# The low part of the split weights of the last feed-forward: by an adding GpSimd transfer instead of a VectorE subtraction

## Chip, core and metric

The kernel runs on one core of a Trainium2 chip. The metric is the time of one execution on the device in microseconds (us); the time of a kernel is the median over its runs. Engines in the rows: PE is TensorE (PEld its weight loads), DVE is VectorE, ACT is ScalarE, POOL is GpSimd, SP is SyncE (SPq the queue that issues the loads).

## The reference, cut to what matters

One sequence of 512 tokens with 1024 features, in float32, goes through a first block (mixed attention and a feed-forward) and then a second block of two layers. Each layer of the second block ends in a feed-forward with 4096 hidden features; behind the last one stands a norm, which is the result:

```python
def sq_relu_mlp(h, w1, w2):
    return jnp.square(jax.nn.relu(h @ w1)) @ w2
...
        x = x + g2 * sq_relu_mlp(modulate(rms_norm(x, norm2_g[l]), sh2, sc2), w_mlp1[l], w_mlp2[l])
...
    return rms_norm(x, final_norm_g)
```

In the last layer (`l == 1`) the feed-forward has this one stream of 512 tokens.

## The kernel before

**Split products.** TensorE multiplies in `float32r`, which keeps fewer bits than float32. Each operand is therefore held as a high part, rounded to `float32r`, and a low part, the rest, and each product is made as three (`mm3`, lines 128 to 131): high weights with high tokens (L129), low weights with high tokens (L130), high weights with low tokens (L131).

**Weights.** `load_w` (lines 109 to 119) brings one weight tile of 128 x 1024 float32 (512 KB): SyncE loads it into `wstage` (L116), ScalarE copies it into `whi` (L117), and VectorE subtracts, `wlo = wstage - whi` (L118). On the lane "main" there are two buffers for `wstage` and three for `whi` and `wlo` each, handed out in the order of the program: a tile takes the buffers of the tile three before it, and waits until TensorE has read them for the last time.

**The last feed-forward** (`mlp`, from line 226). The 4096 hidden features are worked on in 8 groups of 512. A group has eight weight tiles, called A0 to A3 and B0 to B3 here. A0 to A3 are tiles of `w1`: 24 products of 512 columns each give 128 hidden features (`d`), which ScalarE takes through ReLU, square and the copy `uh` (L256, L260, L261) and VectorE into the low part `ul` (L262). B0 to B3 are tiles of `w2`: each gives two output tiles of 128 features, with the four hidden tiles of the group as inputs (`uh`, `ul`), 24 products again, and VectorE adds them to the residual stream (`area`, L287). 64 weight tiles in all. In the first group A0 to A2 go over the first 256 tokens and then the second 256, because the second half's norm comes later. In the last group B2 and B3 are done in halves of 256 tokens too, so that the final norm can start.

**What sets the order.** Nothing is ordered by hand here. A scheduler places all instructions on the engines' queues by priority and by a model of their times, and within an engine they run in that order; each waits for semaphores. `d` banks are seven in the last layer. GpSimd has the softmax's subtraction in the attention before (L744) and the final scaling (L1305), and issues no transfers.

Of the kernel before, what the change touches and what calls it, by code (L numbers as in the profile page):

```python
# [10 lines left out]
F32 = mybir.dt.float32  # L11
# [4 lines left out]
OP = mybir.AluOpType  # L16
# [12 lines left out]
# the parts that the tokens of a stream (0: x, 1: context) are worked on in where a norm would hold up the rest  # L29
# [17 lines left out]
def kernel(ctx: ExitStack, tc: tile.TileContext, A, out, dbg=None):  # L47
# [36 lines left out]
    # ---------------------------------------------------------------- helpers  # L84

    # Buffers of one name are handed out in program order. Work that shall overtake other work needs its own: a lane.
# [22 lines left out]
    def load_w(src, n, cuts=()):  # L109
        ln = lane[lane[""]]  # L110
        wst, width = ln["wst"], ln["width"]
        st = wst.tile([128, width], F32, name="wstage", bufs=ln.get("stage"))
        hi = wst.tile([128, width], F32R, name="whi", bufs=ln.get("split"))
        lo = wst.tile([128, width], F32R, name="wlo", bufs=ln.get("split"))
        for a, b in zip((0, *cuts), (*cuts, n)):
            nc.sync.dma_start(st[:, a:b], src[:, a:b])  # L116
            act.activation(hi[:, a:b], st[:, a:b], AF.Copy)  # L117
            dve.tensor_sub(lo[:, a:b], st[:, a:b], hi[:, a:b].bitcast(F32))  # L118
        return hi, lo

    def after(cur, prev):
        """cur is issued behind prev on the same engine."""
# [10 lines left out]
    def split(hi, lo, src, scale=None, shift=None):  # L133
        """hi + lo = src * scale + shift, each exact in float32r."""
# [16 lines left out]
    def rstd_steps(srcs, n, width, psum, name="n", parts=None, gains=None, ending=1):  # L151
        """In two pieces, the steps for the first sources and a call for the rest and the result:
        1 / sqrt(mean over features + eps), on every partition; srcs: [128, n] feature tiles. With parts: a list of
        calls, one per part of the tokens, that give it. With gains: of y = rms_norm(src) * gain, rms_norm(y) being
        src * gain times what the first such list gives, and y src * gain times what the second gives."""
# [18 lines left out]
        def rest():  # L174
            for sl in parts:
                for i in range(together, len(srcs)):
                    add(i, sl)
                if gains:
                    # 1 / (r1 r2)^2 = mean((x gain)^2) + eps / r1^2
# [26 lines left out]
    def normed(hT, srcs, rstd, scale, shift=None):  # L206
        """hT[k] (hi, lo) = srcs[k] * rstd * scale[k] (+ shift[k])"""
# [5 lines left out]
    def normed_stream(hT, v, psum, gain, shift, ending, rest=None):  # L213
        """normed for a whole stream, one part of its tokens after the other"""
# [5 lines left out]
    def by_parts(n_tiles, units, lead):  # L220
        """Order of work of weight tiles on units of tokens: the first tiles go through unit after unit, so that
        later units can still be on their way."""
# [3 lines left out]
    def mlp(streams, w1, w2, pool_u, psum, side=None, rstd=None, ending=1):  # L226
        """x[m] += gate(m) * (relu(h @ w1)^2 @ w2)[m] for each stream (x, hT, n, gate); h = hT (* rstd)"""
        parts = [PARTS[0 if st[2] == S else 1] for st in streams]
        for g in range(32 // GRP):
# [34 lines left out]
            # towards the end the tokens' parts come one after the other, for the norm behind  # L264
# [6 lines left out]
            for mb, mm, ci, sl in steps:  # L271
                if mb not in ws:
                    # the last weights have buffers of their own: the others are for what comes next
# [18 lines left out]
    # ---------------------------------------------------------------- residual streams  # L292
    # The first block needs its input for its first norm and again where it adds to it; in between, the memory
    # of the residual stream serves the modulations.
# [3 lines left out]
    # ---------------------------------------------------------------- work on the second block's weights alone  # L298
# [3 lines left out]
    def filling(behind=0):  # L302
        """Work for when nothing else is ready."""
# [5 lines left out]
    # shift1, norm1_g * (1 + scale1), gate1, shift2, norm2_g * (1 + scale2), gate2; one column per feature tile  # L309
# [5 lines left out]
    def modulations(held, passing, scratch, behind=None):  # L315
        """silu(c) @ w_mod + b_mod for both condition vectors, by products and sums along the free axis."""
# [42 lines left out]
    def filters(fp, psum, which):  # L359
        """Spectra of the long convolutions at the odd half frequencies, cosine and sine parts."""  # L360
# [78 lines left out]
    # ---------------------------------------------------------------- second block, one stream at a time  # L439
# [10 lines left out]
    def mixers(lq, n):  # L450
        """Fourier input, convolution gate, convolution input"""
        return [[lq.tile([128, n], F32, name=f"{nm}{i}") for i in range(2)] for nm in ("F", "x0_", "z")]

    def front_norm(pi, ps, l, v, rest=None):
        """Normed and modulated input."""
# [18 lines left out]
    def front(pi, ps, l, v, lat, mixin, hT):  # L474
        """The input's projections and their latents."""
# [13 lines left out]
        # the convolution's inputs come last: until then their tiles are free  # L489
# [35 lines left out]
        def conv(i, p, dst):  # L525
            """dst = short convolution of channel tile i along tokens"""
# [113 lines left out]
    def values(ap_, ps, l, key_lats):  # L640
        """Values of all heads, token-major."""
# [17 lines left out]
    def attention(ap_, sm, l, v, key_lats, lat, ps, es=None, lp=None, fill=()):  # L659
        """Latent attention of stream v over the keys of key_lats; its output, transposed, in four tiles, which may  # L660
        take the memory of the latents in lp. fill: pieces of other work on the tensor engine."""
# [5 lines left out]
        # the rotary rows of the keys are the same for every head  # L667
# [9 lines left out]
        def heads(j, ps):  # L677
            """queries and keys of a pair of heads"""
# [88 lines left out]
        # behind the rest of the attention in order: for when nothing of it is ready  # L767
# [6 lines left out]
    def out_half(l, half, src, v, ps):  # L774
        """x += gate * (four of the mix tiles) @ w_out"""
# [3 lines left out]
    def out_pieces(l, half, src, v, ending=4):  # L779
        """out_half in pieces, each with the pool of its sums' bank; those of the last weight tiles one part of the  # L780
        tokens after the other"""
# [26 lines left out]
    def side_lane(wrk, width=0, stage=0, split_=0, banks=3):  # L808
        """A lane of its own, with weight buffers where width is given."""
# [8 lines left out]
    def second_block_prologue(ph, ps):  # L818
        """Work that the first block's output has no part in: modulations, filters, the context's first layer
        up to its feed-forward. In pieces, for between the groups of the first block's feed-forward."""  # L820
# [5 lines left out]
        def side(g, j, load):  # L826
            at = 4 * g + j
            if at == BL:
                # the new schedule begins with weights at hand
# [64 lines left out]
    # ================================================================ block 1  # L894
    with ExitStack() as ph:
# [5 lines left out]
        # the norm's 1 / rms is applied to the projections  # L901
# [19 lines left out]
        # gated linear attention operands: bq, bk, br  # L921
# [32 lines left out]
        # relative position tables f_h(e - 127), kept in DRAM  # L954
# [13 lines left out]
        # values and gate inputs, token-major: av | cv | bv | ba  # L968
# [25 lines left out]
        # twelve causal heads; two per tile  # L994
        def head_pairs():
            for j in range(6):
# [6 lines left out]
                if j == 5:  # L1003
                    # all projections are made: the memory of their input is free
# [6 lines left out]
                for i in range(4):  # L1011
# [3 lines left out]
                    for h2 in range(2):  # L1015
                        h_ = 2 * j + h2
                        r = slice(64 * h2, 64 * h2 + 64)
                        # once the linear attention is through, its buffers serve every second head
                        other = gla_done and h2
                        p = ps1.tile([128, 512], F32, name="g" if other else "s")  # L1020
                        # float32r products of under 256 columns take longer than those of 256
# [31 lines left out]
        # log decay, cumulative within each 128-token tile, on [(head, key channel), token]  # L1053
# [34 lines left out]
        # Within a tile, a key meets a query at the level at which they part into the halves of one block: the decay  # L1088
        # between them is the product of the key's up to the middle and the query's from there. Level 0 is the diagonal.
# [7 lines left out]
        # the queries of a level, each head's in its own rows and columns: one product takes all heads  # L1097
# [49 lines left out]
        # states before tiles 1..3  # L1147
# [366 lines left out]
```

## Time and profile before

| | |
|---|---|
| runs | 2357.88 and 2352.8 us, median 2355.34 |
| profiled execution | span 2353.3 us (the page gives no other time of it) |
| busy in the span | TensorE 97%, VectorE 62%, ScalarE 42%, GpSimd 6% |
| share of the chain that ended last | TensorE 87%, VectorE 6%, DMA 3%, ScalarE 2% |
| transfers | 248.52 MB, all issued by SyncE but 0.4% of the engines' time |

The page sums up an execution; the share of an engine is an average over stages. The last feed-forward takes from about 1980 us to 2338 us of the span, the final norm the rest. What decides there is which wait ends last ahead of a product of TensorE, since TensorE has no gap between its products.

### The profile page before, as it was taken

What the parts mean: (1) busy time and instruction counts of PE and PEld (TensorE: products, weight loads), DVE (VectorE), ACT (ScalarE), POOL (GpSimd) and SP (SyncE); (2) the same over time, 40 slices, a digit from 0 to 9 for tenths busy, and PEclk for the clock granted to TensorE, in tenths of its full rate; (3) what the DMA queues carried; (4) which work ended last, traced back from release to release, by engine and by line L of the source; (5) the groups of instructions that cost most, each with busy time, mean ns of one, the idle gap of its engine ahead of it and who ended that gap; (6) DMA issues with size and microseconds to landing.
All of it is one profiled execution on the core that took longest, in us unless ns stands there. A gap on an engine that the chain in (4) does not pass through costs nothing.

```text
span 2353.3 us, 32927 instructions
## 1 busy us (share of the span) xinstructions
PE 2287.6 (97%) x12907; PEld 1898.1 (81%) x12907; DVE 1469.5 (62%) x2641; ACT 996.0 (42%) x1717; POOL 137.0 (6%) x173
## 2 busy tenths in 40 slices
PE   8999999999999999899999999999899999999997
PEld 7866677778877788788988888888878788888886
DVE  7888778576666684766785554533755666443345
ACT  5344553344344452654533322343443644333333
POOL 0022200000000000321000000000001220000000
PEclk9999999999999999999999999999999999999999
DMA  6523454434331422102354442321222101332232
GB/s 232 166 76 131 130 166 151 164 134 141 126 100 63 149 82 72 54 19 75 106 180 152 152 152 72 103 90 59 83 89 73 41 28 46 107 99 98 90 99 72
DMA packets 78853, 248.52 MB, mean 106 GB/s; under 512 B 9342, under 2 KB 13872, under 8 KB 77930
## 3 DMA queue, kind: packets, MB, share of 16 engines
q1 hardware_dynamic: 78698, 246.42, 31.9%
q8 instruction: 102, 1.67, 0.3%
q14 instruction: 53, 0.43, 0.1%
HBM read 241.63 MB, written 4.75 MB: 105 GB/s over the span
## 4 chain that ended last, share of the span: by engine, by line
PE 87%; DVE 6%; DMA 3%; ACT 2%; issue 1%; POOL 0%; SPq 0%; DVEq 0%; ACTq 0%; POOLq 0%
PE d L129 23%; PE d L130 22%; PE d L131 22%; PE o L760 3%; PE t L750 2%; DVE wlo L118 1%; PE s L129 1%; PE s L131 1%; DMA area<-in_wmod_dram 1%; PE e L129 1%; PE s L130 1%; PE e L429 1%; PE o L1042 1%; PE e L130 1%; PE e L131 1%
## 5 line engine op out<-in xcount | busy, mean ns | idle before, releaser
L117 ACT ACTIVATE whi<-wstage 128x1024 fp32r<-128x1024 f32 (+4 forms) x318 | 324.6, 1024 | 511.0 <-PE d L131 426.3
L118 DVE TENSOR_TENSOR wlo<-wstage,whi 128x1024 fp32r<-128x1024 f32 (+4 forms) x318 | 378.0, 1191 | 256.2 <-ACT whi L117 253.5
L129 PE MATMUL d<-uh,whi 128*128 128x512 f32 (+1 forms) x1056 | 380.4, 361 | 1.3 <-ACT uh L261 1.3
L130 PE MATMUL d<-uh,wlo 128*128 128x512 f32 (+1 forms) x1056 | 379.8, 360 | 0.0
L131 PE MATMUL d<-ul,whi 128*128 128x512 f32 (+1 forms) x1056 | 374.3, 359 | 0.0
L129 PEld LDWEIGHTS d<-uh,whi 128*128 128x128 f32 x1056 | 198.5, 188 | 33.8 <-ACT uh L261 2.2
L131 PEld LDWEIGHTS d<-ul,whi 128*128 128x128 f32 x1056 | 198.9, 188 | 32.4 <-issue 1.5
L130 PEld LDWEIGHTS d<-uh,wlo 128*128 128x128 f32 x1056 | 198.7, 188 | 30.9 <-issue 1.3
L287 DVE SCALAR_TENSOR_TENSOR area<-d,mod,area 128x512 f32<-128x512 f32 (+1 forms) x134 | 95.4, 725 | 145.2 <-PE d L131 145.1
L256 ACT ACTIVATE w<-d 128x256 f32<-128x256 f32 (+1 forms) x96 | 50.4, 525 | 215.9 <-PE d L131 209.2
L338 DVE SCALAR_TENSOR_TENSOR w<-wm,cb 128x1024 bf16<-128x1024 f32 x96 | 114.9, 1220 | 25.7 <-DMA wm<-in_wmod_dram 25.5
L262 DVE TENSOR_TENSOR ul<-w,uh 128x512 fp32r<-128x512 f32 (+1 forms) x128 | 79.3, 622 | 19.9 <-ACT uh L261 19.8
L338 DVE SCALAR_TENSOR_TENSOR mj<-area,area 128x1024 bf16<-128x1024 f32 x64 | 79.7, 1246 | 6.9 <-DMA area<-in_wmod_dram 6.1
L739 DVE TENSOR_REDUCE mx<-s 128x1 f32<-128x768 f32 x64 | 61.2, 956 | 33.6 <-PE s L131 32.8
L260 ACT ACTIVATE w<-w 128x512 f32<-128x512 f32 (+1 forms) x128 | 73.0, 570 | 6.5 <-DVE w L258 5.6
L261 ACT ACTIVATE uh<-w 128x512 fp32r<-128x512 f32 (+1 forms) x128 | 73.9, 577 | 3.5
L744 POOL TENSOR_SCALAR sb<-sb,mx 128x768 f32<-128x768 f32 x64 | 57.9, 906 | 207.7 <-DVE mx L740 80.4
L760 PE MATMUL o<-pt,V 128*64 128x128 f32 x768 | 64.9, 281 | 0.0
L285 DVE TENSOR_TENSOR area<-d,area 128x512 f32<-128x512 f32 (+1 forms) x66 | 44.2, 672 | 31.4 <-PE d L131 31.1
L750 PE MATMUL t<-c_ident,sb 128*128 128x128 f32 x384 | 60.7, 281 | 0.8 <-ACT pt L753 0.7
L674 POOL CAST k000h<-kr0h 32x512 fp32r<-32x512 f32 x2 | 1.7, 844 | 1017.9 <-PE d L625 1017.9
L287 DVE SCALAR_TENSOR_TENSOR ctx<-d,mod,ctx 128x256 f32<-128x256 f32 x64 | 30.8, 481 | 48.0 <-PE d L131 47.8
(1185 smaller groups left out, 5761.0 us busy)
## 6 DMA issues: line engine op xcount, KB each, us to landing
wstage<-in_w_m_dram SPq DMA_DIRECT2D x128, 512.0 KB, 3.5
wstage<-in_w_ff_dram SPq DMA_DIRECT2D x64, 512.0 KB, 4.2
wm<-in_wmod_dram SPq DMA_DIRECT2D x64, 512.0 KB, 4.2
wstage<-in_w_in_dram SPq DMA_DIRECT2D x56, 512.0 KB, 3.4
area<-in_wmod_dram SPq DMA_DIRECT2D x32, 512.0 KB, 4.2
wstage<-in_w_out_dram SPq DMA_DIRECT2D x32, 512.0 KB, 3.5
wstage<-in_w_v_dram SPq DMA_DIRECT2D x8, 520.0 KB, 4.2
ktab<-in_kt_dram SPq DMA_DIRECT2D x16, 256.0 KB, 2.7
```

Of the source, the lines that this page charges most:

```text
L117: act.activation(hi[:, a:b], st[:, a:b], AF.Copy)
L118: dve.tensor_sub(lo[:, a:b], st[:, a:b], hi[:, a:b].bitcast(F32))
L129: pe.matmul(ps, lhsT=whi, rhs=xhi, start=start, stop=False)
L130: pe.matmul(ps, lhsT=wlo, rhs=xhi, start=False, stop=False)
L131: pe.matmul(ps, lhsT=whi, rhs=xlo, start=False, stop=stop)
L260: act.activation(u, r, AF.Square)
L261: act.activation(uh, u, AF.Copy)
L262: mark[g, j] = dve.tensor_sub(ul, u, uh.bitcast(F32))
L287: dve.scalar_tensor_tensor(x[m][:, sl], ps, gate(m), x[m][:, sl], op0=OP.mult, op1=OP.add)
L338: after(dve.scalar_tensor_tensor(t, w, 1.0, sv[v], op0=OP.mult, op1=OP.mult, accum_out=mraw[l][v][j // 8][:, j % 8:j % 8 + 1]), behind)
L750: pe.transpose(pt[:, (kk - a) * 128:(kk - a + 1) * 128], sb[:, kk * 128:(kk + 1) * 128], ident)
L760: last_[h2] = after(pe.matmul(po[64 * h2:64 * h2 + 64, q], lhsT=V[kk][:, 64 * h_:64 * h_ + 64], rhs=PT[h2][:, kk * 128:(kk + 1) * 128], st ...
```

## The change

In the last layer's feed-forward, from its first weight tile on, the low part is made in two steps. ScalarE writes minus the high part into `wlo`: a copy of `wstage` with scale -1, rounded to `float32r` on the way. Then GpSimd issues a transfer that reads the same 512 KB from the weights in DRAM a second time and adds them onto what stands in `wlo`. VectorE's subtraction is gone for these 64 tiles. The number of buffers and the loads of SyncE stay. Comments were taken out as well, so the lines of the changed kernel are numbered 5 to 7 higher (L120 is the new activation, L121 the new transfer, L134 to L136 the three products).

```diff
         for a, b in zip((0, *cuts), (*cuts, n)):
             nc.sync.dma_start(st[:, a:b], src[:, a:b])
             act.activation(hi[:, a:b], st[:, a:b], AF.Copy)
-            dve.tensor_sub(lo[:, a:b], st[:, a:b], hi[:, a:b].bitcast(F32))
+            if ln.get("adding"):
+
+                act.activation(lo[:, a:b], st[:, a:b], AF.Copy, scale=-1.0)
+                nc.gpsimd.dma_start(lo[:, a:b], src[:, a:b], accum_op=OP.add)
+            else:
+                dve.tensor_sub(lo[:, a:b], st[:, a:b], hi[:, a:b].bitcast(F32))
...
             streams = [(xs[v], hT, N_OF[v], lambda m, v=v: mod[l][v][5][:, m:m + 1]) for v, hT in hs.items()]
+            if last:
+                lane["main"]["adding"] = True
             mlp(streams, A[f"w2_m1{l}"], A[f"w2_m2{l}"], pu, ps, None if last else layer1_prologue(ph, ps),
```

The scheduler sees other waits and orders some instructions anew. ScalarE, second group, from the ReLU of A3 on, before (`whi` of B2, B3 and of the next group's first tiles; in brackets the semaphores waited for):

```order
L256 ACTIVATE w_19361<-d_19334 128x512 [waits DVE_49,PE_49]
L117 ACTIVATE whi_19436<-wstage_19435 128x1024 [waits DMAHW1_49]
L260 ACTIVATE w_19363<-w_19361 128x512 [waits Activation_49]
L261 ACTIVATE uh0_19359<-w_19363 128x512 [waits Activation_49]
L117 ACTIVATE whi_19470<-wstage_19469 128x1024 [waits DMAHW2_49,DVE_49,PE_49]
L117 ACTIVATE whi_19504<-wstage_19503 128x1024 [waits DMAHW3_49,DVE_49,PE_49]
```

The same place in the changed kernel:

```order
L120 ACTIVATE wlo_19451<-wstage_19449 128x1024 [waits DMAHW1_49,DMASW3_49,PE_49]
L261 ACTIVATE w_19373<-d_19346 128x512 [waits DVE_49,PE_49]
L117 ACTIVATE whi_19450<-wstage_19449 128x1024
L265 ACTIVATE w_19375<-w_19373 128x512 [waits Activation_49]
L266 ACTIVATE uh0_19371<-w_19375 128x512 [waits Activation_49]
L120 ACTIVATE wlo_19486<-wstage_19484 128x1024 [waits DMAHW2_49,DMASW4_49,PE_49]
L117 ACTIVATE whi_19485<-wstage_19484 128x1024 [waits PE_49]
L120 ACTIVATE wlo_19521<-wstage_19519 128x1024 [waits DMAHW3_49,DMASW5_49,PE_49]
L117 ACTIVATE whi_19520<-wstage_19519 128x1024 [waits PE_49]
```

The negative high part stands ahead of the ReLU of the w1 tile and ahead of the same tile's `whi`.

TensorE, second group, end of B0 and start of B3, before (B0 is 19368, B1 19402, B2 19436, B3 19470):

```order
L131 MATMUL d_19387<-ul0_19360,whi_19368 128x512
L129 MATMUL d_19407<-uh0_19359,whi_19402 128x512
...
L131 MATMUL d_19455<-ul0_19360,whi_19436 128x512
L129 MATMUL d_19475<-uh0_19242,whi_19470 128x512 [waits Activation_49]
L130 MATMUL d_19475<-uh0_19242,wlo_19471 128x512 [waits DVE_49]
```

In the changed kernel (B0 is 19380, B1 19415, B2 19450, B3 19485, the next group's A0 19520):

```order
L136 MATMUL d_19400<-ul0_19372,whi_19380 128x512
L134 MATMUL d_19421<-uh0_19371,whi_19415 128x512
...
L136 MATMUL d_19470<-ul0_19372,whi_19450 128x512
L134 MATMUL d_19491<-uh0_19251,whi_19485 128x512 [waits Activation_49]
L134 MATMUL d_19505<-uh0_19251,whi_19485 128x512 [waits DVE_49]
L134 MATMUL d_19526<-h00h_18547,whi_19520 128x512 [waits DVE_49,Activation_49]
L135 MATMUL d_19491<-uh0_19251,wlo_19486 128x512 [waits DMASW7_49]
```

Two products with high weights of B3 and A0 now stand ahead of the first one with B3's `wlo`, and that one waits for GpSimd's transfer (DMASW). Between B0's last product (d_19400) and it lie 33 products; B0's tile ends at the 42nd product of the w2 phase, B1's `wlo` is first read at the 20th, the last `uh` at the 37th. GpSimd's queue has the 64 transfers one behind the other between the last softmax subtraction and the final scaling:

```order
L121 DMA wlo_19381<-in_w2_m21_dram 128x1024 [waits DMASW1_49,Activation_49]
L121 DMA wlo_19416<-in_w2_m21_dram 128x1024 [waits DMASW2_49,Activation_49]
L121 DMA wlo_19451<-in_w2_m21_dram 128x1024 [waits DMASW3_49,Activation_49]
L121 DMA wlo_19486<-in_w2_m21_dram 128x1024 [waits DMASW4_49,Activation_49]
L121 DMA wlo_19521<-in_w2_m11_dram 128x1024 [waits DMASW5_49,Activation_49]
```

Each waits for ScalarE's write of minus the high part, and for the transfer eight before it.

## Rows read from the trace of the kernel before

**Rows 1.** The page's first part: busy us, share of the span, instructions of each engine.
```profile
span 2353.3 us, 32927 instructions
...
PE 2287.6 (97%) x12907; PEld 1898.1 (81%) x12907; DVE 1469.5 (62%) x2641; ACT 996.0 (42%) x1717; POOL 137.0 (6%) x173
```
**Rows 2.** Stretches: length, each engine's busy us (count), granted clock, DMA share, GB/s.
```profile
2000.00:2100.00 100.00, 100.00 (x435) 81.28 (x434) 41.31 (x47) 36.79 (x51) 0.00 (x0) 1.00 0.33 106
...
2200.00:2300.00 100.00, 100.00 (x434) 81.26 (x433) 39.86 (x44) 32.33 (x44) 0.00 (x0) 1.00 0.29 95
```
**Rows 3.** Timeline of ScalarE, one w1 tile: start, us, engine, line, operation [idle, releaser].
```profile
2121.40 0.60 ACT L256 ACTIVATE w<-d 128x512 f32<-128x512 f32 x1 [4.49 <-PE d L131]
...
2123.49 0.64 ACT L261 ACTIVATE uh<-w 128x512 fp32r<-128x512 f32 x1
...
2127.00 0.60 ACT L256 ACTIVATE w<-d 128x512 f32<-128x512 f32 x1 [2.88 <-PE d L131]
```
**Rows 4.** TensorE's waits, 1940 to 2000 and 2000 to 2353: us, times, longest.
```profile
PE n L191 <- DVE nw L202: 3.1, 1, 3.1
PE d L129 <- ACT h00h L136: 0.9, 1, 0.9
...
PE n L191 <- DVE nw L202: 2.0, 1, 2.0
```
**Rows 5.** Groups of instructions, 1996 to 2338: busy us, mean ns | idle before, releaser.
```profile
L118 DVE TENSOR_TENSOR wlo<-wstage,whi 128x1024 fp32r<-128x1024 f32 x61 | 74.5, 1223 | 122.4 <-ACT whi L117 122.4
...
L117 ACT ACTIVATE whi<-wstage 128x1024 fp32r<-128x1024 f32 x61 | 64.3, 1056 | 120.2 <-PE d L131 119.9 <-DMA wstage<-in_w_m_dram 0.3
...
L130 PEld LDWEIGHTS d<-uh,wlo 128*128 128x128 f32 x272 | 51.0, 188 | 10.1
```
**Rows 6.** Timelines of ScalarE, VectorE and TensorE at the stage's start.
```profile
1975.51 1.06 ACT L117 ACTIVATE whi<-wstage 128x1024 fp32r<-128x1024 f32 x1 [0.42 <-PE d L131]
...
1976.47 0.40 ACT L163 ACTIVATE nw<-area 128x256 f32<-128x256 f32 x1
...
1976.60 1.22 DVE L118 TENSOR_TENSOR wlo<-wstage,whi 128x1024 fp32r<-128x1024 f32 x1 [0.60 <-ACT whi L117]
...
1979.01 0.70 PE L191 MATMUL n<-nw,ones 128*128 128x256 f32 x2 [3.10 <-DVE nw L202]
...
1981.82 0.41 PE L130 MATMUL d<-h00h,wlo 128*128 128x256 f32 x1
```
**Rows 7.** Timeline of GpSimd up to the end.
```profile
2341.01 2.68 POOL L1305 TENSOR_TENSOR area<-area,rstd 128x256 f32<-128x256 f32 x3 [393.37 <-DVE rstd L203]
```
**Rows 8.** Timelines of TensorE and ScalarE where a buffer comes free.
```profile
2102.25 0.40 PE L129 MATMUL d<-uh,whi 128*128 128x512 f32 x1
...
2102.45 1.06 ACT L117 ACTIVATE whi<-wstage 128x1024 fp32r<-128x1024 f32 x1 [6.04 <-PE d L131]
```
**Rows 9.** The loading line, 1900 to 2353: issue ns min/median/max; landing.
```profile
L116 SPq DMA_DIRECT2D wstage<-in_w_m_dram x64: 327/328/328, 1952.7 to 2312.9; - x64
...
DMA to landing us min/median/max: 3.3/3.5/4.5
```
**Rows 10.** Timeline of TensorE, 256-column products of the last group.
```profile
2326.47 0.28 PE L129 MATMUL d<-uh,whi 128*128 128x256 f32 x1
2326.59 0.28 PE L130 MATMUL d<-uh,wlo 128*128 128x256 f32 x1
```
**Rows 11.** Timelines of ScalarE and TensorE at the first group's fourth w1 tile.
```profile
1996.39 0.60 ACT L256 ACTIVATE w<-d 128x512 f32<-128x512 f32 x1 [3.83 <-PE d L131]
...
1999.43 0.39 PE L130 MATMUL d<-h00h,wlo 128*128 128x512 f32 x1
```
**Rows 12.** Stretches at the stage's start, columns as in rows 2.
```profile
1976.00:1980.50 4.50, 0.70 (x2) 0.30 (x2) 3.80 (x8) 2.32 (x7) 0.00 (x0) 1.00 0.33 96
1980.50:1984.00 3.50, 3.42 (x15) 3.39 (x16) 3.50 (x10) 2.44 (x7) 0.00 (x0) 0.51 0.06 26
```
**Rows 13.** DMA queues, 1985 to 2320: packets, MB, share of 16 engines.
```profile
q1 hardware_dynamic: 8496, 30.94, 28.3%
```

## The prediction

> **What bounds the kernel now.** I read the engine totals first, then the stretches of the last feed-forward, then TensorE's waits there, then the split line by line, and last the instants at which a weight buffer comes free and is needed. TensorE is busy for 97% of the span, VectorE for 62% [rows 1]. In the last feed-forward TensorE is busy for the whole of each 100 us, 434 or 435 products each, so one 512-column product takes 0.230 us and one weight tile (24 products) 5.53 us; on ScalarE the ReLUs of two tiles start 5.6 us apart [rows 2, 3]. From 1940 us on TensorE waits three times, always at a norm, 3.1 + 0.9 + 2.0 = 6.0 us; never for a `wlo` [rows 4]. So VectorE's subtraction, 1223 ns for each tile, lies beside the products, as does ScalarE's `whi` of 1056 ns [rows 5].
>
> **The change part by part.** *Removed:* 64 subtractions on VectorE, 64 x 1.22 = 78 us of its time. No product waits for one, so this gives nothing in the steady part. The one that stands near a critical chain is at 1976.60, ahead of the sum of squares that TensorE awaits at 1979 [rows 6]. There ScalarE now has two activations instead of one ahead of the square at 1976.47, so the norm loses about 1.0 us on ScalarE where it wins 1.2 on VectorE: nothing, to about half a us.
>
> *Added on ScalarE:* 64 x 1.06 = 68 us. In each 100 us it is busy for 36.8 [rows 2]; 18 tiles add 19. In a w1 tile the new activation stands ahead of the ReLU, so `uh` comes 1.06 us later; the product that first needs the last `uh` is the 37th of the w2 phase, 36 x 0.230 = 8.3 us after the w1 tile's end, and `uh` is ready after some 4 us (2.7 from the ReLU's start to the end of `uh` [rows 3], 1.06 and the hand-over before it). Hidden; were that cover gone, 1 us a group.
>
> *Added on GpSimd:* 64 transfers. GpSimd is idle for 393 us until the final scaling [rows 7], so nothing queues behind a waiting transfer but the next ones. SyncE's loads keep their order. But the chain from a free buffer to a ready `wlo` is longer. Before: 0.2 us from the last product that reads a buffer to ScalarE (2102.25 to 2102.45) [rows 8], then two engine operations. Now: 0.2 + 1.06 (negative high part) + 0.05 + D, and the weight load of 0.19 ahead of the product [rows 5], together 1.5 + D, where D is the time from GpSimd's issue to landing. **D is the unknown**: no GpSimd transfer and no adding one is in this trace. The nearest row is SyncE's load of the same 512 KB: 3.5 us to landing (3.3 to 4.5) [rows 9]. Lower bound 3.5, one such load. Upper bound 10.5, three of them end to end: source read, target read, target write, or a plain load in between. I take 7.0, two, since the sum needs two operands fetched and the loads of the next tiles go on beside it.
>
> What can be late, by place (buffers rotate by three):
> - *Ordinary tile.* Free to needed: two tiles, 11.1 us, so D up to 9.6 is hidden.
> - *Fourth w2 tile (B3).* It takes B0's buffer. By the new order 33 products lie between B0's last and B3's first `wlo`, 33 x 0.230 = 7.6 us; D up to 6.1 is hidden. At 7.0 TensorE waits 0.9, in seven groups: **6.3 us**.
> - *B3 of the last group.* 6 products of 512 columns and 46 of 256 (0.118 each, [rows 10]) give 6.8 us; D up to 5.3 is hidden: **1.7 us**.
> - *Fourth w1 tile of the first group (A3).* Its buffer is free at about 1996.4, its `wlo` is needed at 1999.43 [rows 11]. 1996.4 + 1.06 + 0.05 + 7.0 + 0.2 = 2004.7: **5.3 us**.
> - *Third w1 tile of the first group.* ScalarE starts on it at 1975.51, TensorE reads it at 1981.82 [rows 6]; 1975.51 + 1.06 + 0.05 + 7.0 + 0.2 = 1983.8: **2.0 us**.
> - *Clock.* After the 4.5 us in which TensorE had 0.7 us of work (1976 to 1980.5), its granted clock was 0.51 for 3.5 us, which is the 1.2 GHz level, where the stage has 1.00 [rows 2, 12]; the 15 products there took 0.22 each instead of 0.118, 1.5 us more. The wait at A3 is as long, so once more **1.5 us**.
>
> Sum 6.3 + 1.7 + 5.3 + 2.0 + 1.5 = 16.8, some 17 us. The profiled span is 2353.3; the page gives no other time of that execution, and the two timed runs (2352.8 and 2357.88) lie 0.5 below to 4.6 above it, their median 2.0 above. 2353.3 + 17 + 2.0 = **2372 us**, +0.7%. At D = 3.5 only A3 is late, 1.8 us, which gives 2357.
>
> The loads in this stage take 28.3% of the transfer engines' time [rows 13]. An adding transfer of the same bytes with two reads and a write costs at most three times a load, so 57 to 113% in all; at twice, 85%, it still fits.
>
> **The rivals.** *Slower, every tile late.* From D = 9.6 on each tile waits, since its `wlo` can't start before the tile three before is through. At D = 10.5: B3 waits 4.4 a group, the second w2 tile 2.3 (its buffer is free 5.53 + 18 x 0.230 = 9.7 us before its `wlo` is read, so D up to 8.2 is hidden), a w1 tile 0.9: 7.6 x 7.5 groups = 57; A3 8.8, the third tile 5.5, the clock 1.5: 73 us, so 2428. By rate it comes to the same place: at 113% of the engines a tile takes 6.25 instead of 5.53 us, 64 x 0.72 = 46 us. For it: loads issued after each split run beside the adding transfer, and GpSimd's own share of issuing is unseen. Against: the engines stand at 28%, so 2.5 times a load's cost fits. It decides from D = 9.4, where the sum reaches 47 us.
>
> *Hidden anyway.* If the second operand costs only transfer time and no second landing, D stays under 6. A load's share is 0.283 x 5.53 = 1.57 us of the 3.5; one more of that gives D = 5.1 and only A3's 3.3 us and a fraction at the start: 2359. The Trainium skill states this as a rule (Collectives: The Full Stack, "The bandwidth ceiling: the fold count and why AG ≠ RS ≠ AR"): the add itself costs nothing, the reduction is slower because it needs two source reads, so about half the rate. By that rule the result is this rival's 2359 rather than my 2372; no row here shows an adding transfer.
>
> *A gain.* If the relief of VectorE shortened the norms at both ends, at most the 6.0 us of waits in [rows 4] could go: 2349. Against it: the other activation of ScalarE in the same chain.
>
> *No move of work.* VectorE loses its subtractions by the order of instructions, so the change does what it says; that the stage doesn't feel it is the case "hidden".
>
> **Chances and range.** A measurement of this kernel tells a change from none at about 2%, 47 us. Forecast (D from 6 to 9.4: +5 to +45 us) 0.50; hidden 0.20; a gain 0.03, hardly ever over 2%; every tile late, over 2%, 0.27, about half of it at D up to 10.5. So faster 0.01, same 0.72, slower 0.27. From the hidden case's low end with the spread of runs (2354) to the upper bound of D (2430) about 0.17 is left out: the gain, and slow cases beyond 10.5. The likeliest case alone has 2358 to 2402.
>
> **What would show it.** VectorE some 75 us and ScalarE some 65 us different in the stage, with TensorE waiting for a transfer into `wlo` at A3 once (about 5 us) and at B3 in each group (under 2 us), and at ordinary tiles never. Landing of GpSimd's transfers near 7 us. Waits in all tiles, or a landing over 9.4 us, would show the slower rival; a landing under 6 us with no wait at B3 the hidden one. I am wrong if GpSimd's issue itself takes several us a tile, if the transfers spread over few engines, or if SyncE's loads become late behind the adding ones so that ScalarE waits for `wstage`.

## The result and the profile after

The changed kernel takes 2377.01 us (2376.73 and 2377.28) against 2355.34, a ratio of 1.0083 with a 95% interval of 1.0065 to 1.0101: 19.6 us, +0.8%. Forecast were 2372 us, +0.7%. One execution of a later kernel, quiet, took 3193 us at a granted clock of 0.652 (all the others 0.98 to 0.99) and counts in no ratio below. The page's totals first (columns as in [rows 1]):

```profile
span 2375.4 us, 33118 instructions
...
PE 2299.5 (97%) x12907; PEld 1904.1 (80%) x12907; DVE 1393.9 (59%) x2577; ACT 1055.4 (44%) x1781; POOL 191.9 (8%) x237
```

VectorE lost 75.6 us and 64 instructions, ScalarE has 59.4 us more, GpSimd 54.9: the work moved as the diff says. The span grew by 22.1 us all the same. The waits of TensorE from 1940 us to the end, columns as in [rows 4], which had no line for `wlo`, and above them one of ScalarE:

```profile
ACT wlo L120 <- DMA wstage<-in_w_m_dram: 38.9, 8, 6.1
...
PE d L135 <- DMA wlo<-in_w_m_dram: 11.6, 9, 3.5
PE n L196 <- DVE nw L207: 5.5, 2, 3.5
PE d L134 <- ACT h00h L141: 0.9, 1, 0.9
```

Nine waits for a transfer into `wlo`; the norms' waits are 0.4 us longer. ScalarE, too, now waits for staging loads, eight times, before it writes minus the high part; no wait of TensorE follows from that. The transfers themselves, by the changed kernel's transfer line (issue on GpSimd min/median/max in ns; who waited, us and times; landing):

```profile
L121 POOL DMA_DIRECT2D wlo<-in_w_m_dram x64: 862/862/1019, 1969.0 to 2348.2; - x64
...
  PE d L135: 11.6, 9
...
DMA to landing us min/median/max: 5.2/7.0/10.0
```

The median landing is 7.0 us, as taken. The same line for one transfer each: the first group's fourth w1 tile (A3) and the second group's fourth w2 tile (B3):

```profile
L121 POOL DMA_DIRECT2D wlo<-in_w_m_dram x1: 862/862/862, 2003.6 to 2003.6; - x1
...
DMA to landing us min/median/max: 5.4/5.4/5.4
...
L121 POOL DMA_DIRECT2D wlo<-in_w_m_dram x1: 862/862/862, 2074.8 to 2074.8; - x1
...
DMA to landing us min/median/max: 7.0/7.0/7.0
```

So 7.0 is a mixture: 5.2 to 5.7 at the B2 of the first seven groups, 6.9 to 8.3 at the seven B3 that TensorE waited for, up to 10.0 at the w1 tiles, which have the time. Three of these (9.8, 9.9 and 10.0) lie above the 9.4 us that the prediction took as a sign of the slower rival, and no wait of TensorE is listed for them. The closest is the third w1 tile of the third group, by its transfer line and TensorE's timeline:

```profile
L121 POOL DMA_DIRECT2D wlo<-in_w_m_dram x1: 862/862/862, 2088.4 to 2088.4; - x1
...
DMA to landing us min/median/max: 9.9/9.9/9.9
...
2098.03 0.40 PE L134 MATMUL d<-h00h,whi 128*128 128x512 f32 x1
2098.31 0.50 PE L135 MATMUL d<-h00h,wlo 128*128 128x512 f32 x1
```

It lands just as its first product is due; that one starts 0.28 instead of 0.23 us behind the product before. Around the second group's B3, ScalarE and GpSimd (timelines, columns as in [rows 3]):

```profile
2073.48 1.06 ACT L120 ACTIVATE wlo<-wstage 128x1024 fp32r<-128x1024 f32 x1 [6.06 <-PE d L135]
2074.44 1.04 ACT L117 ACTIVATE whi<-wstage 128x1024 fp32r<-128x1024 f32 x1
2075.39 1.04 ACT L120 ACTIVATE wlo<-wstage 128x1024 fp32r<-128x1024 f32 x1
...
2074.83 0.86 POOL L121 DMA_DIRECT2D wlo<-in_w_m_dram  x1 [8.87 <-ACT wlo L120]
2076.73 0.86 POOL L121 DMA_DIRECT2D wlo<-in_w_m_dram  x1 [1.03 <-ACT wlo L120]
```

B0's buffer comes free at 2073.4, minus the high part is written, the transfer is issued at 2074.83, and the next tile's (A0) 1.9 us behind it. SyncE issues two plain loads of 512 KB in the same stretch, each when `whi` has freed a staging buffer (its loading line, 2074.5 to 2082: first and last start behind the durations):

```profile
L116 SPq DMA_DIRECT2D wstage<-in_w_m_dram x2: 328/328/328, 2075.5 to 2077.4; - x2
```

The first of them comes 0.67 us behind GpSimd's issue, which itself lasts 0.86. That instant sorts the landings. Where the next load is issued within 0.9 us (33 of the 64 transfers, nearly all at 0.67 or 0.68: `whi` stands right behind minus the high part on ScalarE), the landing takes 6.7 to 10.0 us, median 8.3. Where it is issued at 1.16 us (28 transfers: another activation stands between the two), it takes 5.2 to 9.0, median 5.8. Most of them, in both kinds, are issued while the adding transfer before is still in flight, which could lengthen them too; among those issued after it had landed the difference stays: 6.9 to 8.3 for the eight of the first kind, 5.4 to 6.3 for the six of the second. A3 above is of the second kind: loads 1.16 and 3.05 us behind it, the next adding transfer 2.4 us, and yet 5.4.

TensorE at the end of that transfer (timeline):

```profile
2080.89 0.40 PE L134 MATMUL d<-h00h,whi 128*128 128x512 f32 x1
2081.88 0.50 PE L135 MATMUL d<-uh,wlo 128*128 128x512 f32 x1 [0.59 <-DMA wlo<-in_w_m_dram]
2082.21 0.39 PE L136 MATMUL d<-ul,whi 128*128 128x512 f32 x1
```

2074.83 + 7.0 is when the product starts. Its row shows 0.59 us of idle time, but the product could have started at 2080.89 + 0.23 = 2081.12, and the next one comes 0.33 instead of 0.23 us later: the stop costs 0.76 + 0.10 = 0.86. The idle time of a wait understates its price by some 0.27 us, since the rows of products overlap.

The transfer engines from 2010 to 2330 (queues as in [rows 13]; q0 is GpSimd's; then the median landing):

```profile
q0 software_dynamic: 8055, 29.33, 55.1%
q1 hardware_dynamic: 8085, 29.43, 24.7%
...
wstage<-in_w_m_dram SPq DMA_DIRECT2D x56, 512.0 KB, 7.9
wlo<-in_w_m_dram POOLq DMA_DIRECT2D x56, 512.0 KB, 7.0
```

Together 80%, where the sum had 57 to 113%. An adding transfer takes 0.551 x 320 / 56 = 3.15 us of all sixteen engines, a load 1.4. The loads of SyncE land after 7.9 instead of 3.5 us [rows 9].

Where the 22.1 us arose is read from the products themselves: TensorE runs 12,907 in both profiles, and the start of the k-th product in the one less that in the other, both counted from the first product, is the shift there. By the last product ahead of the stage it is already 3.6 us, in instructions that the change does not touch; over the profiles shown here it lies between -5.2 and +4.4 there, so it is the scatter of executions. In the stage 18.5 us are added:

| place | added, us | forecast, us |
|---|---|---|
| norm at the start | 0.4 | 0 to 0.5 |
| third w1 tile of the first group: wait 1.3, and 0.7 of slow clock behind norm and wait | 2.0 | 2.0, all of it wait |
| fourth w1 tile of the first group: wait | 3.7 | 5.3 |
| ... and the slow clock behind it | 2.6 | 1.5 |
| fourth w2 tile, groups one to seven, and small drifts between | 9.5 | 6.3 |
| last group and final norm | 0.2 | 1.7 |
| sum | 18.5 | 16.8 |

### The profile page after: what moved, and what is told of

Same layout as the page of the kernel before. It is cut to its first block, busy times and chain, and to the rows that moved or that the text cites. A ratio compares the mean times of both kernels' runs of the same rounds, so it can differ in the third digit from the quotient of the medians.

```text
span 2375.4 us, 33118 instructions
## 1 busy us (share of the span) xinstructions
PE 2299.5 (97%) x12907; PEld 1904.1 (80%) x12907; DVE 1393.9 (59%) x2577; ACT 1055.4 (44%) x1781; POOL 191.9 (8%) x237
## 4 chain that ended last, share of the span: by engine, by line
PE 74%; issue 13%; DVE 5%; DMA 3%; POOL 2%; ACT 2%; SPq 0%; DVEq 0%; POOLq 0%; ACTq 0%
PE d L134 18%; PE d L135 18%; PE d L136 18%; PE o L765 2%; PE t L755 2%; POOL wlo L121 2%; PE s L134 1%; PE s L136 1%; PE s L135 1%; PE e L134 1%; PE o L1047 1%; DVE wlo L123 1%; PE e L135 1%; PE e L434 1%; PE e L136 1%
## 5 line engine op out<-in xcount | busy, mean ns | idle before, releaser
L134 PE MATMUL d<-uh,whi 128*128 128x512 f32 (+1 forms) x1056 | 378.7, 361 | 0.8 <-ACT uh L266 0.8
L123 DVE TENSOR_TENSOR wlo<-wstage,whi 128x1024 fp32r<-128x1024 f32 (+4 forms) x254 | 299.6, 1182 | 134.0 <-ACT whi L117 131.5
L136 PE MATMUL d<-ul,whi 128*128 128x512 f32 (+1 forms) x1056 | 376.9, 359 | 0.0
L134 PEld LDWEIGHTS d<-uh,whi 128*128 128x128 f32 x1056 | 198.5, 188 | 33.5 <-ACT uh L266 1.7
L136 PEld LDWEIGHTS d<-ul,whi 128*128 128x128 f32 x1056 | 198.9, 188 | 32.0 <-issue 1.5
L120 ACT ACTIVATE wlo<-wstage 128x1024 fp32r<-128x1024 f32 x64 | 67.7, 1058 | 178.9 <-PE d L135 140.0
L121 POOL DMA_DIRECT2D wlo<-in_w_m_dram x64 | 55.4, 866 | 342.5 <-ACT wlo L120 337.1
```

Source lines behind the costliest of these rows:

```text
L121: nc.gpsimd.dma_start(lo[:, a:b], src[:, a:b], accum_op=OP.add)
L134: pe.matmul(ps, lhsT=whi, rhs=xhi, start=start, stop=False)
L136: pe.matmul(ps, lhsT=whi, rhs=xlo, start=False, stop=stop)
```

## The experiments

Each ratio is to the kernel before, timed on the same chip in the same job; "in the stage" is the shift of TensorE's products from the last product ahead of the last feed-forward to the end, in one profiled execution of each kernel.

| run | ratio (95%) | in the stage, us |
|---|---|---|
| the change | 1.0083 (1.0065 to 1.0101) | 18.5 |
| plain | 1.0020 (1.0011 to 1.0028) | 6.1 |
| next_short | 1.0086 (1.0073 to 1.0099) | 18.9 |
| neg_dve | 1.0008 (0.9998 to 1.0017) | 1.8 |
| tight_sub | 1.0021 (1.0011 to 1.0031) | 6.1 |
| load_short | 1.0044 (1.0030 to 1.0058) | 9.8 |
| both_short | 1.0057 (1.0045 to 1.0070) | 10.0 |
| wlo4 | 1.0192 (1.0178 to 1.0206) | 42.4 |
| first_sub | 1.0033 (1.0020 to 1.0046) | 8.2 |
| quiet | 1.0023 (1.0010 to 1.0036) | 1.2 |
| w4s4 | 1.0048 (1.0035 to 1.0061) | 7.6 |
| more_load | 1.0167 (1.0147 to 1.0187) | 39.8 |
| w4s4_first | 1.0010 (1.0001 to 1.0019) | 3.5 |

### plain: the same chain without the add

```diff
-                nc.gpsimd.dma_start(lo[:, a:b], src[:, a:b], accum_op=OP.add)
+                nc.gpsimd.dma_start(lo[:, a:b], src[:, a:b])
```

> All 64 transfers stay on GpSimd with the same order of instructions, but they only write the weights and add nothing; the low part is left wrong. Theory A (the add costs a second read of the same length, and the landing is what it costs): landing falls from 7.0 to 3.5 to 5 us; the waits at the fourth w2 tile (7.0 us in seven places, 9.5 with what follows them) are gone, at the first group's fourth w1 tile 1 to 3 us stay; time 3 to 6 us over before. Rival B (the path over GpSimd is slow by itself, whatever the transfer does): landing stays near 7 us, the time stays about 18 us over before.

The transfer line of this kernel from 2026 to 2330 (as above), then its queues from 2010 to 2330, then TensorE's waits from 1940 to the end:

```profile
L121 POOL DMA_DIRECT2D wlo<-in_w_m_dram x55: 527/527/530, 2027.0 to 2326.6; - x55
...
DMA to landing us min/median/max: 3.6/4.0/7.8
```

```profile
q0 software_dynamic: 8352, 30.42, 32.1%
```

```profile
PE d L135 <- DMA wlo<-in_w_m_dram: 1.8, 1, 1.8
```

The landing falls to 4.0 us, the waits at B3 are gone, only A3's stays. So A, and not B: without the add a transfer over GpSimd lands after 4.0 us, near the 3.5 of SyncE's loads before; the add makes the difference. A plain GpSimd transfer takes 0.321 x 320 / 58 = 1.77 us of all engines, the adding one 3.15, 1.8 times as much. The rule of the Trainium skill that the rival "hidden anyway" went by (Collectives: The Full Stack, "The bandwidth ceiling: the fold count and why AG ≠ RS ≠ AR": about half the rate, for two source reads) is stated there for a reduction between cores; the ratio of 1.8 agrees with it.

### next_short and load_short: what shares the engines at B3

next_short shortens A0's adding transfer, which is issued behind B3's:

```diff
-                nc.gpsimd.dma_start(lo[:, a:b], src[:, a:b], accum_op=OP.add)
+                c = b if next(ln["tiles"]) else a + 64
+                nc.gpsimd.dma_start(lo[:, a:c], src[:, a:c], accum_op=OP.add)
...
-                lane["main"]["adding"] = True
+                lane["main"].update(adding=True, tiles=iter([g == 0 or j > 0 for g in range(8) for j in range(8)]))
```

> Order of instructions unchanged on every engine; only the adding transfer of the first w1 tile of groups two to eight, which GpSimd issues 1.9 us behind that of the fourth w2 tile, brings 64 of its 1024 columns (the other columns of that tile's low part are left as minus the high part). Theory A1 (an adding transfer alone lands in 5.3 us, and the 7.0 at the fourth w2 tile is made by the next adding transfer that shares the engines with it): landing at the fourth w2 tile falls to 5.3 to 6.0, its seven waits of 7.0 us go to under 1 us; time 8 to 10 us over before, all of it in the first group. Rival A2 (7 us is the length of that transfer at this place, from the plain loads beside it): landing there stays 6.8 to 7.3, the seven waits stay, time about 18 us over before.

load_short shortens the two plain loads:

```diff
-            nc.sync.dma_start(st[:, a:b], src[:, a:b])
-            act.activation(hi[:, a:b], st[:, a:b], AF.Copy)
+            c, e = next(ln["tiles"]) if ln.get("adding") else (b, b)
+            nc.sync.dma_start(st[:, a:c], src[:, a:c])
+            act.activation(hi[:, a:c], st[:, a:c], AF.Copy)
+            if c < b:
+                act.activation(hi[:, c:b], ln["fixed"][:, c:b], AF.Copy)
...
+                    (64 if g and j in (1, 2) else 1024, 64 if g and j in () else 1024)
+                    for g in range(8) for j in range(8)]))
```

> Order of the products unchanged; in groups two to eight the plain loads of the second and third w1 tile bring 64 of 1024 columns (ScalarE takes the other columns of both parts from a constant tile, so those weights are wrong). Every adding transfer is whole. These two loads are the ones that SyncE issues while the adding transfer of the fourth w2 tile is in flight. Theory A2 (plain loads beside it make 7.0 us out of the 5.3 of an undisturbed one): landing at the fourth w2 tile of groups one to seven 5.3 to 5.9 us, its waits under 1 us in all, time 8 to 11 us over before. Rival A3 (7 us at this place has another cause, such as the tile or the state of GpSimd's queue): landing stays 6.8 or more and the time 18 to 20 us over before.

(Minus the high part is taken from the same constant, and the whole weight is added onto it, so the two parts still sum to the weight; the expectation says otherwise.) The second group's B3 in next_short and then in load_short, by the transfer line:

```profile
L122 POOL DMA_DIRECT2D wlo<-in_w_m_dram x1: 862/862/862, 2073.5 to 2073.5; - x1
...
DMA to landing us min/median/max: 7.3/7.3/7.3
```

```profile
L125 POOL DMA_DIRECT2D wlo<-in_w_m_dram x1: 865/865/865, 2067.1 to 2067.1; - x1
...
DMA to landing us min/median/max: 5.7/5.7/5.7
```

A1, which I held, fell: with the next adding transfer cut to a sixteenth B3 still lands after 6.8 to 8.7 us and the loss stays whole. With the two loads cut to a sixteenth, and issued at the same 0.7 and 2.6 us behind it as before, it lands after 5.5 to 5.8 at all seven places, TensorE waits for no transfer from 2020 us on, and 8.7 of the 18.5 us in the stage are gone. What makes 7.0 out of 5.5 is the plain loads, which start when the same split frees the staging buffers. By the landings sorted above it would be the first of the two, being issued before GpSimd is through; a run that moves that load back by half a us was not made.

### both_short: both neighbours cut

The edit of load_short with `j in (0,)` in the second condition.

> As load_short, and the adding transfer of the first w1 tile brings 64 columns too. Theory A2: no different from load_short at the fourth w2 tile (5.3 to 5.9 us, time 8 to 11 us over before), since that transfer stands behind it in GpSimd's queue. Rival A1 (both kinds of neighbour share in it): landing and waits fall further than in load_short, by 0.5 us or more a tile.

B3 lands after 5.4 to 5.8 us, as in load_short, and the stage has 10.0 us more than before, against 9.8. Its ratio of 1.0057 is above what was expected; the intervals of the two overlap, and the stage shows no reason. So A0's transfer does not matter for B3's. It matters the other way: A0's 32 KB land after 3.9 to 5.0 us here, and after 6.0 to 8.2 in next_short, where the two loads are whole.

### neg_dve: ScalarE's half of the change alone

```diff
-                nc.gpsimd.dma_start(lo[:, a:b], src[:, a:b], accum_op=OP.add)
+                dve.tensor_add(lo[:, a:b], st[:, a:b], lo[:, a:b].bitcast(F32))
```

> ScalarE writes minus the high part as in the change, but VectorE adds the staged weights onto it; GpSimd issues nothing. Theory A (ScalarE's second activation is hidden): within 1 us of before, no wait for a low part; at most 0.4 us at the norm at the start. Rival C (the added work of ScalarE and the new order are part of the loss): 3 us or more over before, with waits of TensorE for ScalarE or VectorE at the fourth w2 tile.

No wait for a low part; 64 more activations on ScalarE cost nothing in the steady part. In the stage 1.8 us are added, a little over the 1 us of A and under C's 3: 0.4 at the norm and 1.3 right behind it. The stretch 1984 to 1990 of the kernel before and of this one (columns as in [rows 2]) shows the second part:

```profile
1984.00:1990.00 6.00, 6.00 (x53) 6.00 (x52) 6.00 (x17) 3.02 (x7) 0.00 (x0) 1.00 0.00 0
```

```profile
1984.00:1990.00 6.00, 5.12 (x24) 4.83 (x23) 5.99 (x16) 3.66 (x10) 0.00 (x0) 0.54 0.15 59
```

Here the granted clock is 0.54, the 1.2 GHz level; before, that level ended at 1984 [rows 12]. With a wait at the norm of 3.5 instead of 3.1 us the slow stretch is about twice as long. The wait's length alone does not set this: in first_sub (below) TensorE waits 3.1 us there as before, and yet the clock is low for as long (its wait, then a stretch):

```profile
PE n L196 <- DVE nw L207: 3.1, 1, 3.1
...
1981.00:1987.00 6.00, 4.53 (x17) 3.81 (x18) 5.90 (x16) 3.19 (x8) 0.00 (x0) 0.50 0.22 87
```

There it costs 0.6 us in all. What decides the length is not shown.

### tight_sub, first_sub and quiet: subtraction back at chosen tiles

All three take the choice from a list, one entry a tile:

```diff
-            if ln.get("adding"):
+            if ln.get("adding") and next(ln["tiles"]):
...
-                lane["main"]["adding"] = True
+                lane["main"].update(adding=True, tiles=iter([not (j == 7 or g == 0 and j in (2, 3)) for g in range(8) for j in range(8)]))
```

> 54 of the 64 tiles as in the change; subtracted on VectorE as before are the fourth w2 tile of each of the eight groups and the third and fourth w1 tile of the first. Theory A (the loss lies only where a buffer is free late): 0 to 1.5 us over before, no wait for a transfer, though 84% of the transfers remain. Rival D (the load on the transfer engines costs everywhere): at least 8 us over before, with waits at other tiles.

first_sub has `g > 0`, quiet `g > 0 and j < 7` in the list.

> The first group's eight tiles are subtracted on VectorE, the other 56 made as in the change. Theory A (the terms add): the start's 8.7 us and the first group's 2.4 us at its fourth w2 tile are gone, the 7.1 us at the fourth w2 tile of groups two to seven stay: 7 us over before. Rival E (the waits at the fourth w2 tile are an echo of the late start): 0 to 3 us over before, with waits there under 0.2 us.

> 49 of the 64 tiles by the adding transfer; by VectorE as before the whole first group and the fourth w2 tile of the other seven groups, the places where TensorE was seen to wait. Theory A (loss only where a buffer is free late against its landing): no wait for a transfer, within 1 us of before, although the transfers still take some 70% of the engines' time. Rival D (traffic costs by itself): 5 us or more over before.

tight_sub has one wait for a transfer, at the first group's B0 (TensorE's timeline, and that transfer):

```profile
2006.77 0.80 PE L135 MATMUL d<-uh,wlo 128*128 128x512 f32 x1 [3.00 <-DMA wlo<-in_w_m_dram]
```

```profile
L121 POOL DMA_DIRECT2D wlo<-in_w_m_dram x1: 865/865/865, 1999.1 to 1999.1; - x1
...
DMA to landing us min/median/max: 7.7/7.7/7.7
```

The seven waits and both at the start are gone, as A has it, but the first group's tight place has moved on by one tile: 5.9 us with the slow clock behind it, so the expectation of at most 1.5 was wrong. In first_sub six waits of 4.1 us in all stay at B3 of groups two to seven, and 8.2 us in the stage: they are no echo of the start, and the terms add (7 expected). quiet, with 49 adding transfers, has one wait left:

```profile
PE d L135 <- DMA wlo<-in_w_m_dram: 0.6, 1, 0.6
```

and 1.2 us in the stage. Its ratio says 5.4 us. The profile is of its fastest execution (2351.8 us; the others reach 2365.3), and what the others lost where is not shown. That the traffic costs by itself is not seen in the stage, but by these times rival D's 5 us are not excluded; w4s4_first below, with 56 transfers, speaks against them.

### wlo4, w4s4 and w4s4_first: more lead

```diff
-        lo = wst.tile([128, width], F32R, name="wlo", bufs=ln.get("split"))
+        lo = ln.get("lows", wst).tile([128, width], F32R, name="wlo", bufs=ln.get("split"))
...
-                lane["main"]["adding"] = True
+                lane["main"].update(adding=True, lows=ph.enter_context(tile_pool(name="lows", bufs=4)))
```

> The change with a fourth buffer for the low part, in a pool of its own. Theory A (late is only what has its buffer free late): no wait at the fourth w2 tile, none at the first group's fourth w1 tile; landings still 5 to 10 us; time 0 to 4 us over before (the third w1 tile's wait and the norm may stay). Rival D (the doubled traffic costs in itself): 8 us or more over before.

This was the largest miss: 45 us slower. TensorE's waits, and ScalarE at one of them (timeline):

```profile
PE d L134 <- ACT uh L266: 17.7, 7, 3.1
PE d L135 <- DMA wlo<-in_w_m_dram: 10.6, 6, 3.8
```

```profile
2110.48 1.05 ACT L117 ACTIVATE whi<-wstage 128x1024 fp32r<-128x1024 f32 x1
2115.94 1.06 ACT L120 ACTIVATE wlo<-wstage 128x1024 fp32r<-128x1024 f32 x1 [4.42 <-DMA wstage<-in_w_m_dram]
2116.91 0.61 ACT L265 ACTIVATE w<-w 128x512 f32<-128x512 f32 x1
2117.55 0.63 ACT L266 ACTIVATE uh<-w 128x512 fp32r<-128x512 f32 x1
```

The buffer is free earlier, so the next tile's minus-high stands ahead of the square and of `uh` on ScalarE, and waits 4.4 us for its staging load; TensorE waits for that `uh`. w4s4 gives the loads their lead as well:

```diff
+                more = ph.enter_context(tile_pool(name="more", bufs=1))
+                lane["main"].update(adding=True, stages=more, stage=4, lows=more, lo=4)
```

> Four buffers for the low part (as in the run with a fourth one, which lost 46 us) and four instead of two staging buffers, all in a pool of their own; in the steady groups ScalarE's order is that of the run with the fourth low buffer. Theory F (that run lost because minus the high part stands on ScalarE ahead of the ReLU and waits there for a staging load; with two more staging buffers the load is there in time): the 17.7 us of waits for uh fall under 2 us, those at the fourth w2 tile are gone too, time 0 to 6 us over before. Rival G (loads and adding transfers together are too slow for any lead to help): ScalarE still waits for the staging load in every group, time 20 us or more over before.

What ended ScalarE's idle time ahead of line 120, 2040 to 2345 us, in wlo4 and then in w4s4:

```profile
  DMA wstage<-in_w_m_dram: 151.7, 29
```

```profile
  PE d L135: 140.3, 46
```

In w4s4 no staging load is waited for there, TensorE has no wait from 2024 to 2345 us, and from the end of the first group's w1 tiles on the shift grows by only 0.5 us, with whole traffic and landings up to 9.6 us there. F's mechanism holds; the time is over its 0 to 6 us, 7.6 in the stage and 11.3 by the ratio (the profile is of the fastest execution). The 7.6 us lie at the start: TensorE waits 4.0 instead of 3.1 us for the norm, 3.6 instead of 0.9 for `h00h`, where the new activations stand ahead of the norm's on ScalarE, and 3.0 for transfers. w4s4_first takes the list `g > 0` to it:

> The run with four low and four staging buffers, with the first group's eight tiles subtracted on VectorE as before; 56 tiles keep the adding transfer. Theory A (what is left of that run's 7.6 us in this stage, nearly all of it ahead of the second half of the first group, is the start's): no wait for a transfer; -1 to 2 us against before in the stage. Rival D (the doubled traffic of 56 tiles costs by itself): 5 us or more, spread over the groups.

No wait for a transfer at all; 0.1% slower than before (0.2 to 4.5 us, so under rival D's 5). In the stage 3.5 us, 2.9 of them by the first group's first products, where TensorE waits 5.0 instead of 3.1 us for the norm; so more than expected, but no wait for a transfer is in it. No version here is faster than the kernel before.

### more_load: the engines full

```diff
             nc.sync.dma_start(st[:, a:b], src[:, a:b])
+            if ln.get("adding"):
+                nc.sync.dma_start(ln["more"].tile([128, width], F32, name="more", bufs=2)[:, a:b], src[:, a:b])
```

> The change, and SyncE loads each weight tile of this stage a second time into a buffer that nobody reads: one more plain load of 1.57 us of all engines for each tile, so 80% + 28% = 108% of their time if TensorE kept its pace. Theory A2 (landing grows by what runs beside it, and from 9.4 us on every tile is late): landing 9 to 12 us, waits at nearly every tile, 46 to 110 us over before, TensorE paced by the transfers. Rival H (extra plain loads only fill gaps, since adding and plain ones hardly overlap): landing up to 8 us, at most 30 us over before.

Inconclusive on the threshold: the loss of 39 us is under A2's range and over H's. The extra loads were not paced by the tiles but ran ahead. Two stretches of this run, with and without them (columns as in [rows 2]):

```profile
2040.00:2180.00 140.00, 134.16 (x565) 106.37 (x564) 25.03 (x35) 66.12 (x82) 19.85 (x23) 0.99 1.04 318
2240.00:2340.00 100.00, 99.07 (x427) 79.72 (x426) 17.81 (x26) 49.76 (x63) 15.54 (x18) 1.00 0.79 187
```

With the engines full, at 318 GB/s, TensorE was still busy for 134 of 140 us (137 in the change), with landings of 6.6 to 10.4 us in the groups concerned. 27.6 of the 39.8 us in the stage had come by the second group already.

## Why the prediction was right, point by point

- **Place and mechanism** held: the chain of free buffer, minus-high, transfer is longer than the cover at B3 of groups one to seven, at A3 and at the third w1 tile of the first group, and nowhere else. quiet and w4s4_first take these places away or give them lead, and the waits go but for one of 0.6 us.
- **D = 7.0** is what the median and most B3 show, but my reason for it, two landings of 3.5 end to end, was wrong. At B2, and at B3 with the loads cut, it is 5.2 to 5.8, near what the rival "hidden" worked out (5.1, one more load's engine time); the loads that the same split releases make 7.0 of it (load_short). The right number came of a wrong sum. One D for all tiles was wrong too: it went from 5.2 to 10.0.
- **B3**: 6.3 forecast, 7.0 of idle time and 9.5 of shift. Mis-sized twice: D was 8.2 and 8.3 in two groups, and a stop costs some 0.27 us over its idle time. At D = 7.0 one cost 0.86 us, where 0.9 was worked out.
- **Third w1 tile**: the wait was 1.1 us (1.3 of shift) instead of 2.0, since D was 6.7 there and the norm came 0.4 us later.
- **A3 and the clock**: the wait was shorter (3.7 against 5.3, since D was 5.4 there), the clock dearer. From 2009 to 2016 us the granted clock was 0.60, and twelve products took 0.43 instead of 0.23 us: with the one that had waited 2.6 us, where I took 1.5 from the shorter products of [rows 12].
- **The last B3** cost nothing: no load follows it, and D was 5.5 there.
- **ScalarE and the norm**: hidden in the steady part, as said. The 0.4 us at the norm was in the range; the 1.3 us of slow clock behind it (neg_dve) was not foreseen.
- **The rivals**: three of 64 landings passed the 9.4 us that I took as a sign of the slower one, but all at w1 tiles, and none came late by more than 0.05 us; it did not come. Another sign of being wrong did show, ScalarE waiting for staging loads (38.9 us in all, at A1 of groups two to eight and at one B0), and TensorE lost nothing by it: A1's transfers still land 1.9 to 2.1 us ahead of the first product that reads them. Hidden holds for groups two to eight once B3's landing is undisturbed: of load_short's 9.8 us in the stage 8.6 arise in the first group. A gain was not there: VectorE's 75 us bought nothing.
- **The sum**: 16.8 against 18.5 us in the stage is nearer than its terms. Third tile, A3's wait and last B3 were put 3.8 us too high, the other B3, the clock and the norm 5.4 too low; that these nearly cancel is luck.

## What to carry to other kernels

Where an engine is paced by buffers, a longer chain costs only at the tiles whose buffer comes free late; count the products between the last read of a buffer and the first read of its next content, tile by tile, and price the chain against that. Price a transfer with what the same event releases beside it, not alone. And a deeper buffer for one link of the chain lets its instruction move ahead on an in-order engine, where it then waits for the next link: here that made things twice as bad until the loads got their lead too.

## What the runs showed of the hardware

- An adding GpSimd transfer of 512 KB from DRAM onto SBUF: 0.86 us of issue, 5.2 to 5.8 us to landing at best, 3.15 us of all sixteen engines; without the add 0.53, 4.0 (median) and 1.77.
- A plain load of 512 KB issued 0.67 us behind an adding transfer went with landings of 6.7 us and more of that transfer, one issued 1.16 us behind it with 5.2 to 6.5 in 22 of 28.
- Beside such transfers SyncE's loads of 512 KB landed after 7.9 us (median), 3.5 without them.
- A wait of TensorE of 3.5 instead of 3.1 us went with a slow stretch (granted clock about 0.5) of about twice the length, which cost 1.3 us more (neg_dve); in first_sub a wait of 3.1 us went with one as long.
